# Key norms by one transpose and a row through DRAM, and low rotary keys on 128 partitions, in a diffusion backbone's attention

## Chip, cores and metric

One core of a Trainium2 chip runs the whole program. The metric is device time in microseconds (us) of one execution, as the median of several. Five engines work side by side, each through its own instructions in order: TensorE (PE, with its weight loads shown as PEld), VectorE (DVE), ScalarE (ACT), GpSimd (POOL) and SyncE (SP), which here only issues transfers.

## The reference, cut to what matters

Two layers over 512 latent tokens of width 1024, with 256 context tokens as a prefix. Layer 0 mixes tokens by latent attention with 8 heads, layer 1 by a gated MLP; a squared-ReLU MLP follows each. The change lies in layer 0's attention:

```python
kv = (rmsnorm(ckv, kv_a_norm) @ wkv_b).reshape(B, S, MLA_HEADS, QK_NOPE + V_DIM)
k_nope, v = kv[..., :QK_NOPE], kv[..., QK_NOPE:]
k_pe = jnp.broadcast_to(k_pe[:, :, None, :], (B, S, MLA_HEADS, QK_ROPE))
k = rmsnorm(jnp.concatenate([k_nope, k_pe], axis=-1), k_norm)
...
k_lat = rope_part(k_lat, cos, sin)
...
s = jnp.einsum('bqhd,bkhd->bhqk', qi, k, preferred_element_type=jnp.float32) * scale
p = jax.nn.softmax(s, axis=-1)
return jnp.einsum('bhqk,bkhd->bqhd', p.astype(v.dtype), v)
```

A key has 128 plain dimensions and 64 rotary ones, which all heads share. Each head divides its keys by a norm of its own, one number for each of the 768 tokens (256 context, 512 latent).

## The kernel before, in words

Every product is made from split operands: a float32 value is cut into a high part that the engine's fast format holds and a low part, the rest. A product is three matmuls (high by high, high by low, low by high: `mm3`, lines 80 to 82), and `split` (lines 72 to 76) makes the parts, the high one on ACT and the low one on DVE.

Attention runs from about 107 to 350 us of the span, with three generators for each head or pair of heads. `kv_proj(h)` projects head h's keys and values, token tile by token tile (six tiles of 128), transposes the keys (`kt`, line 265) and splits them into `kh` and `kl`. `q_proj(p)` does the same for the queries of two heads. `scores(h, half)` makes, for a tile of 128 queries, the 128 x 768 scores in one PSUM tile `s`, which has a single buffer: five pairs of matmuls of 384 columns (line 633), of which the last two use the rotary keys, `rh` (high) and `rl` (low). `values(h, half)` transposes the probabilities (`pt`, line 655), splits them into `th` and `tl` and multiplies them with the values into `o`.

The keys are not divided by their norms. Instead the scores are multiplied by `rk`, the reciprocal norms of the 768 keys, which must stand in all 128 partitions since the keys lie along a row of scores. One DVE instruction (line 637) multiplies `s` by `rk` and by the query's factor `rq` and finds the row's maximum; the exponential (ACT, line 640) and the scaling (DVE, line 642) follow. The next block of scores needs the buffer that line 637 reads.

The norms come in columns: `st[:, 2, t]` holds those of token tile t, one for each partition, from a sum of squares (ACT, line 260), an addition (DVE, line 270) and a power (POOL, line 271). Lines 272 to 277 spread them: for each token tile a float32 matmul takes the column, repeated 128 times, as the stationary operand and the identity as the moving one, which writes the column as a row into every partition. Two PSUM tiles of three such matmuls (`rkb`) are copied to `rk` by ACT.

The rotary keys are set up once, before the heads (lines 528 to 537): `kpe` holds them twice side by side, so that the transposed tile `krt` has the 64 dimensions in its lower and again in its upper 64 partitions. `rh` takes all 128 partitions, because the queries' rotary part `sq` has its high half in the lower and its low half in the upper 64. `rl` takes the lower 64 alone and meets only `sq`'s lower half.

What sets the order: a scheduler of the framework puts the instructions of each engine in order by its own estimate of their times, within what the data and the buffers allow. Loads of weights go through SP's queue (line 96), four raw buffers deep, each load behind the split that frees its buffer. A background task (`ada_steps`, lines 154 to 188) loads modulation weights through POOL's queue and sums them on DVE.

Of the kernel before, what the change touches and what calls it, by code (L numbers as in the profile page):

```python
# [9 lines left out]
F32 = mybir.dt.float32  # L10
F32R = mybir.dt.float32r
BF16 = mybir.dt.bfloat16
AF = mybir.ActivationFunctionType
ALU = mybir.AluOpType
AX = mybir.AxisListType

P = 128
# [4 lines left out]
TOK = CTX + SEQ  # L22
NT = TOK // P
NL = SEQ // P
HEADS = 8
NOPE = 128
ROPE = 64
# [19 lines left out]
def hybrid_dit_kernel(  # L47
# [6 lines left out]
    nc = tc.nc  # L54
    PE, ACT, DVE, POOL = nc.tensor, nc.scalar, nc.vector, nc.gpsimd
    SBUF, PSUM = bass.MemoryType.SB, bass.MemoryType.PSUM

    def pool(stack, name, bufs=1, space=SBUF, side="left"):
        return stack.enter_context(tc.tile_pool(name=name, bufs=bufs, space=space, side=side, reuse_waits="tile"))
# [19 lines left out]
    def mm3(o, wh, wl, mh, ml, start, stop):  # L79
        PE.matmul(o, lhsT=wh, rhs=mh, start=start, stop=False)  # L80
        PE.matmul(o, lhsT=wh, rhs=ml, start=False, stop=False)  # L81
        return PE.matmul(o, lhsT=wl, rhs=mh, start=False, stop=stop)  # L82
# [34 lines left out]
    ident = per.tile([P, P], F32, name="ident")  # L117
# [92 lines left out]
    ap_ = pool(att, "att")  # L210
# [2 lines left out]
    cq_h = ap_.tile([P, 3, SEQ], F32R, name="cq_h")  # L213
    cq_l = ap_.tile([P, 3, SEQ], F32R, name="cq_l")
    rh = ap_.tile([P, TOK], F32R, name="rh")
    rl = ap_.tile([ROPE, TOK], F32R, name="rl")
    epk = ap_.tile([P, NT], F32, name="epk")
    cosT = ap_.tile([P, NT, ROPE], F32, name="cosT")
    sinT = ap_.tile([P, NT, ROPE], F32, name="sinT")
# [15 lines left out]
    at = SimpleNamespace()  # L235
    Ks, Vs, Qs, Os = {}, {}, {}, {}
    HALF_T = SEQ // 2

    def kv_proj(h):
        wh, wl = at.W(wkv_b, 0, 2, h * 256, 256, f"wkb{h}")  # L240
        vh = at.hp.tile([P, NT, P], F32R, tag="vh", bufs=3, name=f"vh{h}")
        vl = at.hp.tile([P, NT, P], F32R, tag="vl", bufs=3, name=f"vl{h}")
        kh = at.hp.tile([P, TOK], F32R, tag="kh", bufs=2, name=f"kh{h}")
        kl = at.hp.tile([P, TOK], F32R, tag="kl", bufs=2, name=f"kl{h}")
        rk = at.hp.tile([P, TOK], F32, tag="rk", bufs=2, name=f"rk{h}")
        Ks[h], Vs[h] = (kh, kl, rk), (vh, vl)
        st = at.hp.tile([P, 3, NT], F32, tag="st", bufs=2, name=f"st{h}")
        T = None
        for u in range(3):
            t0 = 2 * u  # L250
            o = at.pm(f"kv{h}{u}").rearrange("p (t n) -> p t n", t=2)
            for j in range(2):
                s = slice((t0 + j) * P, (t0 + j + 1) * P)
                for k in range(2):
                    mm3(o[:, j, :], ckv_h[:, k, s], ckv_l[:, k, s], wh[:, k, :], wl[:, k, :], k == 0, k == 1)
            kn = at.hp.tile([P, 2, NOPE], F32, tag="kn", bufs=2, name=f"kn{h}{u}")
            ACT.copy(out=kn, in_=o[:, :, :NOPE])
            split(o[:, :, NOPE:], vh[:, t0:t0 + 2, :], vl[:, t0:t0 + 2, :])
            for j in range(2):
                ACT.activation(out=junk[:, :NOPE], in_=kn[:, j, :], func=AF.Square, accum_out=st[:, 0, t0 + j:t0 + j + 1])  # L260
            if u != 1:
                T = at.pt(f"kt{h}{u}")
            for j in range(2):
                i = j + 2 * (u == 1)
                PE.transpose(T[:, i * P:(i + 1) * P], kn[:, j, :], ident)
            if u:
                s = slice(0, 512) if u == 1 else slice(512, TOK)
                split(T[:, :s.stop - s.start], kh[:, s], kl[:, s], gqk)
            yield
        DVE.scalar_tensor_tensor(out=st[:, 1, :], in0=st[:, 0, :], scalar=1.0 / QK, in1=epk, op0=ALU.mult, op1=ALU.add)  # L270
        POOL.tensor_tensor(out=st[:, 2, :], in0=st[:, 1, :], in1=mhalf[:, :NT], op=ALU.pow)
        for u in range(2):
            o = at.pt(f"rkb{h}{u}")
            for j in range(3):
                t = 3 * u + j
                PE.matmul(o[:, j * P:(j + 1) * P], lhsT=st[:, 2, t:t + 1].to_broadcast([P, P]), rhs=ident, start=True, stop=True)
            ACT.copy(out=rk[:, u * 384:(u + 1) * 384], in_=o[:, :384])
        yield

    def q_proj(p):  # L280
# [6 lines left out]
        for u in range(2):  # L287
# [4 lines left out]
            for j in range(2):  # L292
# [13 lines left out]
                for h in range(2):  # L306
                    PE.transpose(T[:, h, j * P:(j + 1) * P], qn[:, h, :], ident)
            s = slice(u * HALF_T, (u + 1) * HALF_T)
            split(T, qh[:, :, s], ql[:, :, s])
# [8 lines left out]
            for h in range(2):  # L318
                ACT.copy(out=sq[h][:, s], in_=T[:, h * HALF_T:(h + 1) * HALF_T])
            us = slice(2 * u, 2 * u + 2)  # L320
# [11 lines left out]
    with ExitStack() as ini_stack:  # L332
# [7 lines left out]
        def pt(name):  # L340
            return ps.tile([P, 512], F32, tag="t", bufs=2, name=name)

        def pa(name):
            return ps.tile([P, 512], F32, tag="a", bufs=6, name=name)
# [60 lines left out]
        with ExitStack() as xstack:  # L405
# [12 lines left out]
            for k in range(0, KT, 2):  # L418
                o = pa(f"xct{k}")
# [4 lines left out]
            for k in range(KT):  # L424
                o = pa(f"xt{k}")
# [7 lines left out]
        for t in range(NT):  # L433
            o = rp[0][:, t * P:(t + 1) * P] if t < 2 else rp[1][:, (t - 2) * P:(t - 1) * P]
# [18 lines left out]
        for k in range(KT):  # L453
# [6 lines left out]
            for t in range(NT):  # L460
                a_h, a_l = (ch, cl) if t < 2 else (hh[k], hl[k])
                s = bass.ts(t if t < 2 else t - 2, P)
# [23 lines left out]
        for t in range(NT):  # L486
            st = ini.tile([P, 4], F32, name="kst", bufs=4)
# [7 lines left out]
            o = pt(f"ckt{t}")  # L495
            for j in range(2):
                PE.transpose(o[:, j * P:(j + 1) * P], ck[:, j * P:(j + 1) * P], ident)
            for j in range(2):
                s = slice(t * P, (t + 1) * P)
# [12 lines left out]
        for t in range(NL):  # L512
            o = pa(f"qa{t}")
            for k in range(KT):
                s = bass.ts(t, P)
# [3 lines left out]
            st = ini.tile([P, 4], F32, name="qst", bufs=4)  # L519
# [11 lines left out]
        for u in range(2):  # L531
            o = pt(f"krt{u}")
            for j in range(3):
                PE.transpose(o[:, j * P:(j + 1) * P], kpe[:, 3 * u + j, :, :].rearrange("p a r -> p (a r)"), ident)
            s = slice(u * 384, (u + 1) * 384)
            ACT.copy(out=rh[:, s], in_=o[:, :384])
            DVE.tensor_tensor(out=rl[:, s], in0=o[:ROPE, :384], in1=rh[:ROPE, s].bitcast(F32), op=ALU.subtract)

        drain(kv0)

# [2 lines left out]
    class Norm:  # L543
# [7 lines left out]
        def work(self, i, name):  # L551
            return per.tile([P, HALF_T], F32, tag=("nacc", "nsq")[i], bufs=NB[i], name=name)

        def add(self, k, half):
            name = self.name
            src = xT[:, k, half * HALF_T:(half + 1) * HALF_T]
            if self.acc[half] is None:
# [14 lines left out]
        def spread(self, half, pt):  # L572
            self.rb[half] = pt(f"{self.name}rb{half}")[:, :HALF_T]
            for t in range(2):
                PE.matmul(self.rb[half][:, t * P:(t + 1) * P], lhsT=self.st[half][:, 1, t:t + 1].to_broadcast([P, P]),
                          rhs=ident, start=True, stop=True)

        def apply(self, half, pt):
# [4 lines left out]
            if self.rb[half] is None:  # L583
                self.spread(half, pt)
            s = slice(half * HALF_T, (half + 1) * HALF_T)
            for k in range(KT):
# [17 lines left out]
    with hst as st_:  # L604
# [17 lines left out]
        def scores(h, half):  # L622
            kh, kl, rk = Ks[h]
            rk = rk.rearrange("p (a b) -> p a b", a=2)
            qh, ql, sq, rq_ = Qs[h // 2]
            i = h % 2
            for t in (2 * half, 2 * half + 1):
                s = slice(t * P, (t + 1) * P)
                S = ps.tile([P, 2, 512], F32, tag="s", bufs=PS, name=f"s{h}{t}")
                ops = [(qh[:, i, s], kh), (qh[:, i, s], kl), (ql[:, i, s], kh), (sq[i][:, s], rh), (sq[i][:ROPE, s], rl)]  # L630
                for m, (a, b) in enumerate(ops):
                    for n in range(2):
                        PE.matmul(S[:, n, :384], lhsT=a, rhs=b[:, n * 384:(n + 1) * 384], start=m == 0, stop=m == 4)  # L633
                sm = hq.tile([P, 4], F32, tag="sm", bufs=4, name=f"sm{h}{t}")
                rq = rq_[:, t, i, 2:3]
                e = hq.tile([P, 2, 384], F32, tag="p", bufs=5, name=f"p{h}{t}")
                DVE.tensor_tensor_reduce(out=e, in0=S[:, :, :384], in1=rk, op0=ALU.mult, op1=ALU.max, scale=rq,  # L637
                                         scalar=-3.0e38, accum_out=sm[:, 0:1])
                DVE.tensor_scalar(out=sm[:, 1:2], in0=sm[:, 0:1], scalar1=-1.0, scalar2=None, op0=ALU.mult)  # L639
                ACT.activation(out=e, in_=e, func=AF.Exp, bias=sm[:, 1:2], accum_out=sm[:, 2:3])  # L640
                DVE.reciprocal(out=sm[:, 3:4], in_=sm[:, 2:3])
                DVE.tensor_scalar(out=e, in0=e, scalar1=sm[:, 3:4], scalar2=None, op0=ALU.mult)  # L642
                Pr[h, t] = e.rearrange("p a b -> p (a b)")
# [185 lines left out]
    with ExitStack() as st_:  # L829
# [7 lines left out]
        for q in range(4):  # L837
            ws = [W(gm_w_in, 2 * k2, 2, HALF + q * 512, 512, f"gv{q}{k2}") for k2 in range(4)]
            for ts in ((0, 1), (2, 3)) if q == 0 else ((0, 1, 2, 3),):
                acc = {t: (pu if t < 2 else pd)(f"v{q}{t}") for t in ts}  # L840
                for k in range(KT):
                    wh, wl = ws[k // 2]
                    for t in ts:
                        s = slice(t * P, (t + 1) * P)
                        mm3(acc[t], hs[k][0][:, s], hs[k][1][:, s], wh[:, k % 2, :], wl[:, k % 2, :], k == 0, k == KT - 1)
                for t in ts:
# [8 lines left out]
                            in_=gm_bs.rearrange("g p -> (g p)").unsqueeze(0).to_broadcast([P, G * P]))  # L855
        for g4 in range(2):
            o = pt(f"wst{g4}")
# [6 lines left out]
            o = pt(f"rsw{g4}")  # L864
# [121 lines left out]
```

## Time and profile before

| | us |
|---|---|
| median of 3 runs | 1401.54 (1399.29 to 1401.88) |
| the profiled execution | 1399.21 |
| its span | 1397.4 |
| PE busy | 1355.4 |
| DVE busy | 856.0 |
| ACT busy | 545.6 |

The profiled execution is one run; durations and waits below are from it. A busy share tells which engine is full in a stretch; "idle before" and the releaser after an arrow tell what ended a wait. "issue" is time in which an engine waited for nothing that the profile shows. Matmuls are pipelined, so the step from one start to the next is what a matmul costs, not its record's length.

### The profile page before, as it was taken

Reading aid. Unit: us, or ns where it says so; the run is one execution under the profiler, and the core shown is the slowest. Engines: PE = TensorE matmul, PEld = TensorE weight load, DVE = VectorE, ACT = ScalarE, POOL = GpSimd, SP = SyncE. Lnnn points to the kernel's source line nnn. Section 1 sums busy time; section 2 is a strip of 40 time slices with the busy share of each in tenths; the row PEclk is TensorE's granted clock in tenths of the full one; section 3 lists DMA queues with packets and bytes.
Section 4 is the critical chain, followed back from the end, with each engine's and each line's share of the span. In section 5 each row is a group of like instructions: output and inputs, shape, how many; then the busy total and the mean of one; then the engine's idle time right before and its main releaser. Section 6 shows DMA issues by size and latency. Waiting matters only on the chain.

```text
span 1397.4 us, 18421 instructions
## 1 busy us (share of the span) xinstructions
PE 1355.4 (97%) x7159; PEld 1149.3 (82%) x7159; DVE 856.0 (61%) x1423; ACT 545.6 (39%) x1046; POOL 88.7 (6%) x140
## 2 busy tenths in 40 slices
PE   6989899999899999999999999999999999999998
PEld 4878889888898888888898888888888888888888
DVE  5876787887899888543457356555575344343442
ACT  6556556564652231322335233222254133231331
POOL 2031111100011111000000010000000000000000
PEclk9998999999999999999999999999999999999999
DMA  9551221311478878333323332222223222333311
GB/s 286 169 171 35 80 89 41 114 46 39 132 224 277 280 249 272 98 103 99 97 69 102 102 111 86 90 92 91 76 61 121 91 91 91 94 103 93 104 46 61
DMA packets 126823, 163.23 MB, mean 117 GB/s; under 512 B 7467, under 2 KB 111488, under 8 KB 126736
## 3 DMA queue, kind: packets, MB, share of 16 engines
q1 hardware_dynamic: 114784, 119.50, 27.0%
q0 software_dynamic: 11808, 42.03, 9.5%
q8 instruction: 56, 0.92, 0.3%
q10 hardware_dynamic: 144, 0.52, 0.1%
q14 instruction: 31, 0.25, 0.1%
HBM read 159.94 MB, written 2.10 MB: 116 GB/s over the span
## 4 chain that ended last, share of the span: by engine, by line
PE 85%; issue 7%; DVE 3%; DMA 2%; ACT 1%; POOL 1%; SPq 0%; POOLq 0%; DVEq 0%; ACTq 0%
PE s L633 3%; PE v L80 2%; PE v L82 2%; PE v L81 2%; DMA adr<-in_ada_w_dram 2%; PE pt L655 1%; PE wo L80 1%; PE f1d2o L82 1%; PE f1d0o L80 1%; PE f1d0o L81 1%; PE f1d2o L81 1%; PE f1d2o L80 1%; PE f1d0o L82 1%; PE f0d1o L80 1%; PE f0d1o L81 1%
## 5 line engine op out<-in xcount | busy, mean ns | idle before, releaser
L165 DVE SCALAR_TENSOR_TENSOR acc<-adr,sil,acc 128x1024 f32<-128x1024 f32 x70 | 89.7, 1281 | 20.7 <-DMA adr<-in_ada_w_dram 20.0
L161 POOL DMA_DIRECT2D adr<-in_ada_w_dram x80 | 43.4, 542 | 220.9 <-DVE acc L165 122.6
L782 DVE TENSOR_TENSOR f1a<-f1a 128x512 f32<-128x512 f32 (+1 forms) x36 | 22.5, 629 | 39.8 <-ACT f1a L781 39.8
L637 DVE CUSTOM_DVE_ANT_0 p<-s,rk,rq 128x768 f32<-128x768 f32 x32 | 32.5, 1015 | 14.1 <-PE s L633 11.9
L73 DVE TENSOR_TENSOR tl<-pt,th 128x512 fp32r<-128x512 f32 x48 | 32.7, 687 | 11.6 <-ACT th L72 11.2
L72 ACT CAST f0uh<-f0a 128x512 fp32r<-128x512 f32 (+1 forms) x36 | 20.4, 572 | 48.5 <-DVE f0a L782 48.5
L72 ACT CAST th<-pt 128x512 fp32r<-128x512 f32 x48 | 27.9, 589 | 23.6 <-PE o L82 13.6
L640 ACT ACTIVATE p<-p,sm 128x768 f32<-128x768 f32 x32 | 30.1, 940 | 15.1 <-DVE sm L639 15.1
L126 POOL TENSOR_TENSOR nst<-nst,mhalf 128x2 f32<-128x2 f32 x6 | 5.1, 854 | 457.5 <-DVE nst L125 457.5
L73 DVE TENSOR_TENSOR f1ul<-f1a,f1uh 128x512 fp32r<-128x512 f32 (+1 forms) x36 | 22.6, 632 | 18.8 <-ACT f1uh L72 18.6
L782 DVE TENSOR_TENSOR f0a<-f0a 128x512 f32<-128x512 f32 (+1 forms) x36 | 22.5, 627 | 18.4 <-ACT f0a L781 18.4
L72 ACT CAST f1uh<-f1a 128x512 fp32r<-128x512 f32 (+1 forms) x36 | 20.4, 572 | 32.0 <-DVE f1a L782 32.0
L73 DVE TENSOR_TENSOR f0ul<-f0a,f0uh 128x512 fp32r<-128x512 f32 (+1 forms) x36 | 22.4, 627 | 11.7 <-ACT f0uh L72 11.7
L81 PE MATMUL o<-tl,vh 128*128 128x256 f32 x96 | 28.1, 292 | 1.0 <-DVE tl L73 0.9
L80 PE MATMUL o<-th,vh 128*128 128x256 f32 x96 | 28.6, 298 | 0.0
L600 DVE SCALAR_TENSOR_TENSOR xT<-wo,mod,xT 128x512 f32<-128x512 f32 (+1 forms) x40 | 25.1, 638 | 5.2 <-PE wo L82 4.9
L655 PE MATMUL pt<-ident,p 128*128 128x128 f32 x192 | 27.7, 274 | 0.0
L82 PE MATMUL o<-th,vl 128*128 128x256 f32 x96 | 27.1, 282 | 0.0
L655 PEld LDWEIGHTS pt<-ident,p 128*128 128x128 f32 x192 | 22.2, 141 | 1.8 <-issue 1.0
L892 DVE TENSOR_TENSOR gm<-gm,u 128x512 f32<-128x512 f32 x16 | 11.0, 689 | 20.6 <-ACT u L873 20.5
L81 PEld LDWEIGHTS o<-tl,vh 128*128 128x128 f32 x96 | 18.2, 190 | 2.4 <-DVE tl L73 1.7
L642 DVE TENSOR_SCALAR p<-p,sm 128x768 f32<-128x768 f32 x32 | 19.8, 618 | 0.6
(2637 smaller groups left out, 4651.6 us busy)
## 6 DMA issues: line engine op xcount, KB each, us to landing
adr<-in_ada_w_dram POOLq DMA_DIRECT2D x80, 512.0 KB, 4.8
xn<-in_x_dram SPq DMA_DIRECT2D x4, 512.0 KB, 7.2
out_dram<-of SPq DMA_DIRECT2D x8, 256.0 KB, 2.2
xn<-in_ctx_dram SPq DMA_DIRECT2D x2, 512.0 KB, 4.1
ada000r<-in_ada_w_dram SPq DMA_DIRECT2D x1, 512.0 KB
ada001r<-in_ada_w_dram SPq DMA_DIRECT2D x1, 512.0 KB
ada100r<-in_ada_w_dram SPq DMA_DIRECT2D x1, 512.0 KB, 11.3
ada101r<-in_ada_w_dram SPq DMA_DIRECT2D x1, 512.0 KB, 10.2
```

The costliest lines, as they stand in the source:

```text
L72: ACT.copy(out=hi, in_=src)
L73: eng.tensor_tensor(out=lo, in0=src, in1=hi.bitcast(F32), op=ALU.subtract)
L80: PE.matmul(o, lhsT=wh, rhs=mh, start=start, stop=False)
L81: PE.matmul(o, lhsT=wh, rhs=ml, start=False, stop=False)
L82: return PE.matmul(o, lhsT=wl, rhs=mh, start=False, stop=stop)
L161: nc.gpsimd.dma_start(out=r, in_=ada_w[l][k * P:(k + 1) * P, ch * D:(ch + 1) * D])
L165: DVE.scalar_tensor_tensor(out=acc, in0=r, scalar=sil[:, k, 0:1], in1=acc, op0=ALU.mult, op1=ALU.add)
L633: PE.matmul(S[:, n, :384], lhsT=a, rhs=b[:, n * 384:(n + 1) * 384], start=m == 0, stop=m == 4)
L637: DVE.tensor_tensor_reduce(out=e, in0=S[:, :, :384], in1=rk, op0=ALU.mult, op1=ALU.max, scale=rq, scalar=-3.0e38, accum_out=sm[:, 0:1])
L640: ACT.activation(out=e, in_=e, func=AF.Exp, bias=sm[:, 1:2], accum_out=sm[:, 2:3])
L655: PE.transpose(T[:, j, q * P:(q + 1) * P], Pr[h, 2 * half + q][:, (2 * jp + j) * P:(2 * jp + j + 1) * P], ident)
L782: DVE.tensor_tensor(out=f, in0=f, in1=f, op=ALU.mult)
```

## The change

Line 274 now transposes the six columns of norms in one go: 128 x 6 becomes 6 x 128, in float32, by the identity. ACT copies this small tile to SBUF (`rr`), SP writes it to a DRAM tile `rkd` as one row of 768 numbers, and a second transfer reads that row into all 128 partitions of `rk`. The two transfers stand in SP's queue among the weight loads. The low rotary keys `rl` take all 128 partitions, and their matmuls use all 128 rows of `sq`, so the queries' low half now meets the low keys as well.

```diff
-    rl = ap_.tile([ROPE, TOK], F32R, name="rl")
+    rl = ap_.tile([P, TOK], F32R, name="rl")
...
+    rkd = pool(ctx, "rkd", space=bass.MemoryType.DRAM).tile([HEADS, TOK], F32, name="rkd")
...
         POOL.tensor_tensor(out=st[:, 2, :], in0=st[:, 1, :], in1=mhalf[:, :NT], op=ALU.pow)
-        for u in range(2):
-            o = at.pt(f"rkb{h}{u}")
-            for j in range(3):
-                t = 3 * u + j
-                PE.matmul(o[:, j * P:(j + 1) * P], lhsT=st[:, 2, t:t + 1].to_broadcast([P, P]), rhs=ident, start=True, stop=True)
-            ACT.copy(out=rk[:, u * 384:(u + 1) * 384], in_=o[:, :384])
+        o = at.pt(f"rkt{h}")
+        PE.transpose(o[:NT, :P], st[:, 2, :], ident)
+        row = at.hp.tile([NT, P], F32, tag="rr", bufs=2, name=f"rr{h}")
+        ACT.copy(out=row, in_=o[:NT, :P])
+        nc.sync.dma_start(out=rkd[h].rearrange("(t p) -> t p", p=P), in_=row)
+        nc.sync.dma_start(out=rk, in_=rkd[h].unsqueeze(0).to_broadcast([P, TOK]))
...
-            DVE.tensor_tensor(out=rl[:, s], in0=o[:ROPE, :384], in1=rh[:ROPE, s].bitcast(F32), op=ALU.subtract)
+            DVE.tensor_tensor(out=rl[:, s], in0=o[:, :384], in1=rh[:, s].bitcast(F32), op=ALU.subtract)
...
-                ops = [(qh[:, i, s], kh), (qh[:, i, s], kl), (ql[:, i, s], kh), (sq[i][:, s], rh), (sq[i][:ROPE, s], rl)]
+                ops = [(qh[:, i, s], kh), (qh[:, i, s], kl), (ql[:, i, s], kh), (sq[i][:, s], rh), (sq[i][:, s], rl)]
```

The scheduler makes a new order for the whole attention stage. Three places show it. Names carry buffer numbers here, and behind the diff's added lines the code stands one line lower.

PE at head 1, from the norms' spreading to the head's first block of scores, before (`rkb`: spread norms; `pt`: transposed probabilities of head 0; `s`: scores):

```order
L276 MATMUL rkb_1496<-ident,st_1424 128x128 x3
L276 MATMUL rkb_1501<-ident,st_1424 128x128 x3
L655 MATMUL pt_1545<-ident,p_1389 128x128
...
L655 MATMUL pt_1545<-ident,p_1407 128x128
L633 MATMUL s_1592<-kh_1421,qh_1231 128x384 x2
```

and of the change:

```order
L274 MATMUL rkt_1495<-ident,st_1423 6x128
L656 MATMUL pt_1540<-ident,p_1388 128x128
...
L656 MATMUL pt_1540<-ident,p_1406 128x128
L656 MATMUL pt_1555<-ident,p_1388 128x128
...
L656 MATMUL pt_1555<-ident,p_1406 128x128
L634 MATMUL s_1587<-kh_1420,qh_1230 128x384 x2
```

Six matmuls became one transpose, and a second tile of four transposed probabilities moved ahead of the scores.

DVE at head 3, from the split of a weight to the first multiply with the head's norms (L637 before, now L638; printed as ISA), before:

```order
L600 SCALAR_TENSOR_TENSOR xT<-wo_2300,mod,xT 128x512
L73 TENSOR_TENSOR wo02l<-wo02r,wo02h 128x512
L637 ISA p_2320,sm_2319<-s_2308,rk_2111,rq_1894 128x768
L637 ISA sm_2319 128x1
L73 TENSOR_TENSOR tl_2239<-pt_2233,th_2238 128x512
```

and of the change:

```order
L73 TENSOR_TENSOR tl_2226<-pt_2220,th_2225 128x512
L73 TENSOR_TENSOR tl_2241<-pt_2235,th_2240 128x512
L601 SCALAR_TENSOR_TENSOR xT<-wo_2391,mod,xT 128x512
L601 SCALAR_TENSOR_TENSOR xT<-wo_2399,mod,xT 128x512
L73 TENSOR_TENSOR wqb20l<-wqb20r,wqb20h 128x384
L638 ISA p_2307,sm_2306<-s_2295,rk_2102,rq_1885 128x768
L638 ISA sm_2306 128x1
L73 TENSOR_TENSOR tl_2256<-pt_2250,th_2255 128x512
```

Two splits of probabilities, two residual additions and a weight's split now stand ahead of the multiply.

SP's queue at heads 1 to 3 (a piece of the difference):

```order
 L96 DMA wkb4r<-in_mla_wkv_b_dram 128x2x256
+L277 DMA rkd<-rr_1497 6x128
+L278 DMA rk_1422<-rkd 128x768
+L277 DMA rkd<-rr_1766 6x128
+L278 DMA rk_1691<-rkd 128x768
 L96 DMA wo02r<-in_mla_wo_dram 128x2x256
 L96 DMA wqb20r<-in_mla_wq_b_dram 128x384
 L96 DMA wqb21r<-in_mla_wq_b_dram 128x384
 L96 DMA wqb22r<-in_mla_wq_b_dram 128x384
+L277 DMA rkd<-rr_2177 6x128
 L96 DMA wo03r<-in_mla_wo_dram 128x2x256
+L278 DMA rk_2102<-rkd 128x768
```

Each head's write and read stand in line with the weight loads; head 3's read is behind the load wo03r.

## Rows read from the trace of the kernel before

**Rows 1.** The page, part 1: busy us (share of the span) xinstructions

```profile
PE 1355.4 (97%) x7159; PEld 1149.3 (82%) x7159; DVE 856.0 (61%) x1423; ACT 545.6 (39%) x1046; POOL 88.7 (6%) x140
```

**Rows 2.** Stretches: us, busy (xinstructions) PE, PEld, DVE, ACT, POOL; clock, DMA, GB/s

```profile
100.00:125.00 25.00, 21.66 (x116) 20.09 (x116) 15.67 (x49) 13.61 (x50) 3.64 (x3) 0.73 0.20 58
150.00:175.00 25.00, 21.04 (x147) 19.21 (x146) 21.15 (x49) 14.58 (x45) 5.51 (x7) 1.00 0.36 104
...
sum 175.00, PE 174.81 PEld 155.70 DVE 138.70 ACT 98.71 POOL 18.00; mean PE 24.97 PEld 22.24 DVE 19.81 ACT 14.10 POOL 2.57
```

**Rows 3.** Line 633: ns min/median/max, starts; then idle before it (us, times)

```profile
L633 PEld LDWEIGHTS s<-rh,sq x64: 187/188/192, 124.3 to 347.4; 128*128 128x128 f32 x64
L633 PEld LDWEIGHTS s<-rl,sq x64: 182/184/187, 124.9 to 347.9; 64*128 64x128 f32 x64
...
  issue: 7.8, 32
```

**Rows 4.** Order of time on PE, one block: start us, us, instruction [idle before <-releaser]

```profile
252.87 0.51 PE L633 MATMUL s<-kh,ql 128*128 128x384 f32 x2
253.22 0.51 PE L633 MATMUL s<-rh,sq 128*128 128x384 f32 x2
253.66 0.61 PE L633 MATMUL s<-rl,sq 64*128 64x384 f32 x2
254.20 0.38 PE L80 MATMUL o<-th,vh 128*128 128x256 f32 x1
254.42 0.28 PE L81 MATMUL o<-tl,vh 128*128 128x256 f32 x1
254.54 0.28 PE L82 MATMUL o<-th,vl 128*128 128x256 f32 x1
```

**Rows 5.** The same block's weight loads (PEld)

```profile
253.66 0.29 PEld L633 LDWEIGHTS s<-rl,sq 64*128 64x128 f32 x2 [0.25 <-issue]
```

**Rows 6.** Order of time on PE at head 0's and head 3's spread norms

```profile
108.78 2.93 PE L276 MATMUL rkb<-ident,st 128*128 128x128 f32 x12 [0.89 <-POOL st L271]
...
197.37 1.50 PE L276 MATMUL rkb<-ident,st 128*128 128x128 f32 x12
198.70 0.60 PE L655 MATMUL pt<-ident,p 128*128 128x128 f32 x4
199.06 0.48 PE L80 MATMUL wo<-oh,wo01h 128*128 128x512 f32 x1
199.37 0.39 PE L81 MATMUL wo<-ol,wo01h 128*128 128x512 f32 x1
199.60 0.39 PE L82 MATMUL wo<-oh,wo01l 128*128 128x512 f32 x1
```

**Rows 7.** Order of time on PE at head 2: rows after a wait

```profile
163.08 1.60 PE L276 MATMUL rkb<-ident,st 128*128 128x128 f32 x12 [1.91 <-POOL st L271]
...
171.77 0.62 PE L633 MATMUL s<-kh,qh 128*128 128x384 f32 x2 [1.35 <-ACT qh L72]
...
173.43 0.39 PE L81 MATMUL o<-tl,vh 128*128 128x256 f32 x1 [0.69 <-DVE tl L73]
```

**Rows 8.** Transfers: issuer, count, KB each, us to landing; last, the output's writes

```profile
wqa4r<-in_mla_wq_a_dram SPq DMA_DIRECT2D x1, 384.0 KB, 3.2
...
cosT<-in_rope_cos_dram SPq DMA_DIRECT2D x1, 192.0 KB, 9.1
...
bsb<-in_gm_bs_dram ACTq DMA_DIRECT2D x1, 512.0 KB, 5.0
...
DMA to landing us min/median/max: 2.1/2.2/2.9
```

**Rows 9.** Order of time at head 1: SP's load, ACT's copy, DVE's multiply

```profile
140.01 0.37 SPq L96 DMA_DIRECT2D wkb4r<-in_mla_wkv_b_dram  x1
...
140.60 0.48 ACT L277 COPY rk<-rkb 128x384 f32<-128x384 f32 x1 [0.27 <-PE rkb L276]
...
143.66 1.02 DVE L637 CUSTOM_DVE_ANT_0 p<-s,rk,rq 128x768 f32<-128x768 f32 x1 [0.65 <-PE s L633]
```

## The prediction

> **What bounds the kernel now.** I read the page's busy shares first: TensorE (PE) is busy 97% of the span [rows 1]. A share over the whole span says nothing about one stage, so I then read the busy times by stretch. The attention stage, about 107 to 350 us, is where every changed line runs. From 175 to 350 us PE is busy 174.8 of 175 us, while VectorE (DVE) has 138.7 and ScalarE (ACT) 98.7 [rows 2]. So in seven tenths of the stage a microsecond taken off PE is a microsecond off the end, unless something else becomes late. Two stretches are different. From 100 to 125 us PE runs at a granted clock of 0.73, and from 150 to 175 us it has about 4 us of idle time [rows 2]. Next come the rows of the two touched operations, and last the landing times of transfers like the two that are added.
>
> **Low rotary keys on 128 partitions.** This edit looks like nothing: the two matmuls of each block still stream 384 columns. The trace shows that they cost more than their neighbours. In the line's own view the weight loads of the 64-row form sit behind 7.8 us of "issue" time, in 32 of 32 blocks [rows 3]. One block in order of time shows the size. The 128-row pairs of 384 columns start 0.35 us apart (252.87 to 253.22). The next pair, the 64-row one, starts 0.44 us later, at 253.66, and the 256-column matmul behind it another 0.54 us later, at 254.20 [rows 4]. That one itself takes 0.22 us to its follower, where its kin take 0.12 [rows 4]. So the block is late by 0.09 + 0.19 + 0.10 = 0.38 us. Before the 64-row load PE's weight path stood idle for 0.25 us [rows 5]: the loads that normally run under the matmul ahead don't, at the change from 128 rows to 64 and again on the way back. With 128 rows there is no change of form, so I take 32 x 0.38 = **12.2 us** off PE. The bounds are 7.8 us (the booked idle time alone) and twice that.
>
> The Trainium skill, TensorEngine Tiling, Key Properties, says that a change of tiling mode drains the TensorE; the 0.25 us row is what such a drain would look like.
>
> DVE's subtraction into the low keys is twice as many partitions and the same 384 columns. It runs twice in all, so I price it at nothing.
>
> **The norms' broadcast.** Before, each head runs six f32 matmuls, recorded as twelve, in 1.33 us at the full clock (197.37 to the next start at 198.70) [rows 6]. Eight heads are 10.6 us. Head 0's take 2.93 us at the slow clock [rows 6]. I still count 1.33 for it: the matmuls behind it move up into the slow stretch and pay there. The new transpose is one pass over 128 columns. Four such transposes and a 512-column matmul take 0.67 us (198.70 to 199.37), and the 512-column matmul is 0.23, so one transpose is 0.11 us [rows 6], and eight are 0.9 us. That leaves 9.7 us. But its stationary operand has 6 columns, a form that this stage has nowhere else. Its change of form could cost nothing, or as much as the 64-row one. The trace has no clean row for it, and I take the nearest, the 0.38 us of rows 4, for each of eight heads: **3.0 us** back (0 to 3.0). In head 2 the gain is lost. PE waits 1.91 us for GpSimd's power before its matmuls there, and then idles 1.35 and 0.69 us for ACT and DVE within the next 11 us [rows 7]. Finishing earlier only lengthens those waits: **1.2 us** (1.33 - 0.11) back. ACT loses sixteen copies of 0.48 us [rows 9] and gets eight of 6 rows; it is not the bound, and I count nothing.
>
> **The new wait.** In place of two copies from PSUM the row now goes out to DRAM and comes back to all partitions, both on SyncE's queue, the second issued when the first has landed. Who waits is DVE, whose multiply of the scores with the norms (L637) stands in a strict order, and behind it PE, because the scores have a single buffer: the next block of scores starts only when that multiply is done. From the transpose I count 0.3 us for it, 0.4 for ACT's small copy, 2.2 for the write (the output's writes: 2.1 to 2.9), 3.2 for the read (a 384 KB load; a 512 KB broadcast from DRAM took 5.0) [rows 8], and 1.0 for the multiply [rows 9]: 7.1 us, with 2.9 and 5.0 instead 9.6 us. What hides it is PE's own work between the transpose and the second block of scores of that head. The changed order has, for head 1, 20 transposes, 13 matmuls of 384 columns and 13 of 256: 20 x 0.11 + 13 x 0.175 + 13 x 0.118 = 6.0 us. Counted so, heads 3, 5 and 7 have 8.8, 9.1 and 9.1 us; the old order had 4.7, 4.3, 6.6 and 4.3 us. The even heads are projected a whole head ahead of their use (head 2's matmuls run at 163 us [rows 7], its first scores' start at 171.77), and have 10 us or more. So only head 1 stalls, by 7.1 - 6.0 = **1.1 us**; at 9.6 the four odd heads stall by 3.6 + 0.8 + 0.5 + 0.5 = 5.4 us, at less than 6.0 none.
>
> SyncE's queue is passed sixteen times. Ahead of head 1's write stands the load wkb4r, which waited for its buffer until 140.01 us, when head 1's copies were just starting (140.60) [rows 9]: no delay. Behind the new entries stand weight loads; the next one after head 1's and 2's, wo02r, went out only at 170 us before, because its buffer was taken. A few microseconds of blocked queue there are hidden.
>
> **The new order.** Hundreds of PE rows change places in this stage, and a little outside it. DVE has 138.7 us of work in 175 [rows 2]; with some 12 us fewer it is at 85%, and waits like those in rows 7 become more likely. I charge one more such pair, 1.35 + 0.69 = **2.0 us** (0 to 8.0, two more stretches with 4 us idle like 150 to 175).
>
> **Sum.** 12.2 + 9.7 - 3.0 - 1.2 - 1.1 - 2.0 = 14.6 us. The profiled execution took 1399.2 us, 1.8 more than its span, so 1384.6; the median of the three runs lies 2.3 us above that execution, which makes 1386.9. I put the forecast at **1386**.
>
> **Rivals.**
> First, nothing is given back: the six-column form drains nothing, no wait and no reordering costs. Then 12.2 + 9.7 = 21.9 us go, 1377. For it: PE is full, and three of four odd heads have cover. Against it: head 2's idle time is in the trace.
>
> Second, the widened keys bring nothing, because the 0.38 us has another cause than the row count (the last matmul of a block, the bank it closes). Then 14.6 - 12.2 = 2.4 us go: 1396.8, with the median's offset 1399, no change that can be measured. For it: those matmuls are also the last of each block, so position and row count can't be told apart in this trace. Against it: the idle time lies on the load before them as well as behind.
> The Trainium skill, TensorE: Matmul & The Clock Gate, Part 2, has a rule on this side: a weight load's time follows its columns, not its rows. By that rule alone a 64-row matmul costs what a 128-row one does and this is the result; the loads' own lengths agree with it (184 and 188 ns [rows 3]), the idle time ahead of them does not.
>
> Third, slower: the round trip through DRAM outlasts the cover. The deciding point: the gain before stalls is 15.7 us, the four odd heads' cover 33.0 us, so the chain must be (33.0 + 15.7) / 4 = 12.2 us, its two landings 10.5 us instead of 5.4. One load of the start (cosT, 192 KB) did take 9.1 us [rows 8]. With 2.9 and 9.1 the chain is 13.7 us, the stalls 7.7 + 4.9 + 4.6 + 4.6 = 21.8 us, and the time 1399.2 + 6.1 = 1405. Against it: of the transfers in rows 8 only that one, at the start with the queues full, took over 5.0 us.
>
> **How the numbers follow.** Forecast 0.65, first rival 0.14, second 0.10, third 0.11. About 0.2% (2.8 us) is what a measurement of this kernel can tell from no change. Forecast and first rival are faster; the second falls within 0.2%; with a little of the forecast's weak edge moved there, that is 0.79, 0.10, 0.11. The worst of the bounds together, 12.2 + 6.7 - 1.2 - 5.4 - 8.0 = 4.3 us, gives 1395, with the median's offset 1397; the best is 1377. The range 1377 to 1398 leaves out the third rival and the edges.
>
> **What would show it.** In the changed profile: no "issue" time before the low-key matmuls, and 0.35 us from their start to the next (12.2); eight short transposes with or without idle time ahead and behind (3.0); DVE's wait at L637 (now one line lower) for a transfer, long in head 1 and short or none in 3, 5 and 7; PE still full from 175 us on. It is wrong if PE's idle time in 107 to 350 us grows by more than 10 us, or if the low-key matmuls keep their gap.

## The result, and the profile after

The changed kernel takes 1386.37 us (median of 4 runs, 1386.17 to 1387.54), beside 1401.71 us (4 runs) before: a ratio of 0.9897, with a 95% interval of 0.9885 to 0.9910. That is 15.3 us by the medians, 14.4 by the ratio (12.6 to 16.1). The forecast was 1386 in a range of 1377 to 1398. The profiled execution took 1386.22 us, its span 1384.4, 13.0 less than before.

The page's first part, against [rows 1]: busy us (share of the span) xinstructions.

```profile
PE 1335.3 (96%) x7071; PEld 1140.3 (82%) x7071; DVE 852.6 (62%) x1423; ACT 538.7 (39%) x1038; POOL 89.0 (6%) x140
```

PE lost 20.1 us of busy time, but the span only 13.0 us: some of what was freed turned into waiting. The busy times by stretch show where, against [rows 2] (columns as there):

```profile
100.00:125.00 25.00, 17.93 (x101) 16.68 (x101) 17.37 (x55) 14.98 (x59) 4.83 (x6) 0.86 0.29 93
125.00:150.00 25.00, 23.56 (x167) 22.94 (x166) 16.41 (x43) 16.93 (x50) 1.33 (x2) 1.00 0.15 48
150.00:175.00 25.00, 21.62 (x148) 19.72 (x147) 21.50 (x53) 16.09 (x50) 5.72 (x8) 1.00 0.39 118
175.00:350.00 175.00, 171.62 (x1159) 161.37 (x1158) 146.44 (x338) 100.94 (x286) 17.98 (x19) 1.00 0.25 79
```

From 175 to 350 us PE was busy 174.8 of 175 us before and is 171.6 now. (The last 15 us of it are already other work, since the stage ends earlier.) One block of scores on PE, against [rows 4] (start, us, instruction):

```profile
128.40 0.51 PE L634 MATMUL s<-kh,ql 128*128 128x384 f32 x2
128.75 0.51 PE L634 MATMUL s<-rh,sq 128*128 128x384 f32 x2
129.10 0.51 PE L634 MATMUL s<-rl,sq 128*128 128x384 f32 x2
129.45 0.60 PE L317 MATMUL qrt<-ident,qs 128*128 128x128 f32 x4
```

Every pair takes 0.35 us from its start to the next, the low keys' too. That holds beyond this block: before, the step into the low keys' pair has a median of 0.44 us and the step out of it 0.54 over all 32 blocks; both are 0.35 now. Line 634's list of what ended the idle time before it, against [rows 3], has no issue time left, and a wait for DVE's multiply in its place:

```profile
  DVE sm L638: 10.1, 10
  ACT qh L72: 0.3, 1
```

That multiply, line 638, waits for the transfer four times (us, times):

```profile
  DMA rk<-rkd: 9.2, 4
```

Below I compare kernels by stage, since the parts ahead of attention and behind it differ by 1 to 4 us from profile to profile. The marks are starts of instructions in order of time: the first and the last of DVE's 32 multiplies of the scores, and PE's first matmul of the MLP that follows. PE idle is the sum of the gaps on PE between the first and the last multiply. Us, worked out from the traces; the kernels of the lower rows are those of the experiments.

| kernel | start to first multiply | first to last | last to the MLP | MLP to the end | PE idle, first to last |
|---|---|---|---|---|---|
| before | 125.7 | 222.8 | 27.1 | 1021.9 | 4.1 |
| changed | 126.5 | 208.3 | 26.6 | 1023.0 | 8.0 |
| changed, again | 126.4 | 209.1 | 26.6 | 1022.8 | 7.8 |
| wide keys alone | 126.2 | 211.1 | 26.9 | 1021.0 | 3.3 |
| row norms alone | 127.3 | 216.6 | 26.8 | 1028.3 | 6.1 |
| no round trip | 124.7 | 204.4 | 26.9 | 1023.5 | 5.2 |
| transpose on DVE | 122.7 | 206.8 | 24.9 | 1022.1 | 5.7 |

The gain of the change lies in the third column: 14.5 us.

### The profile page after: what moved, and what is told of

Read it like the earlier page. It is cut to its first block, busy times and chain, and to the rows that moved or that the text cites. A ratio compares the mean times of both kernels' runs of the same rounds, so it can differ in the third digit from the quotient of the medians.

```text
span 1384.4 us, 18271 instructions
## 1 busy us (share of the span) xinstructions
PE 1335.3 (96%) x7071; PEld 1140.3 (82%) x7071; DVE 852.6 (62%) x1423; ACT 538.7 (39%) x1038; POOL 89.0 (6%) x140
## 4 chain that ended last, share of the span: by engine, by line
PE 78%; DVE 6%; DMA 5%; issue 5%; ACT 2%; POOL 1%; DVEq 0%; POOLq 0%; ACTq 0%
DMA adr<-in_ada_w_dram 5%; PE s L634 3%; PE v L80 2%; PE v L82 2%; PE v L81 2%; DVE acc L165 2%; PE f1d2o L80 1%; PE f1d0o L81 1%; PE f1d0o L82 1%; PE f1d0o L80 1%; PE f1d2o L81 1%; PE f1d2o L82 1%; PE f1d1o L80 1%; PE f0d2o L80 1%; PE f0d2o L81 1%
## 5 line engine op out<-in xcount | busy, mean ns | idle before, releaser
L638 DVE CUSTOM_DVE_ANT_0 p<-s,rk,rq 128x768 f32<-128x768 f32 x32 | 32.5, 1014 | 13.5 <-DMA rk<-rkd 9.2
L72 ACT CAST th<-pt 128x512 fp32r<-128x512 f32 x48 | 27.1, 587 | 18.8 <-PE o L82 12.6
L82 PE MATMUL o<-th,vl 128*128 128x256 f32 x96 | 27.1, 282 | 0.0
L656 PE MATMUL pt<-ident,p 128*128 128x128 f32 x192 | 26.8, 273 | 0.0
L634 PE MATMUL s<-kh,qh 128*128 128x384 f32 x64 | 17.6, 357 | 4.3 <-DVE sm L638 4.2
```

What stands on the lines that cost most here:

```text
L72: ACT.copy(out=hi, in_=src)
L656: PE.transpose(T[:, j, q * P:(q + 1) * P], Pr[h, 2 * half + q][:, (2 * jp + j) * P:(2 * jp + j + 1) * P], ident)
```

## Experiments

### Each edit alone

The scheduler's order does not depend on the low keys' rows: with wide keys alone the order of PE, DVE, ACT and SP's transfers is that of before, row for row, and with the row norms alone that of the changed kernel. So these two kernels part the edits cleanly.

```diff
-    rl = ap_.tile([ROPE, TOK], F32R, name="rl")
+    rl = ap_.tile([P, TOK], F32R, name="rl")
...
-(sq[i][:ROPE, s], rl)]
+(sq[i][:, s], rl)]
```

> The kernel before with the low rotary keys on 128 partitions and nothing else; the order of TensorE is that of before, row for row. Theory: the change of form between 128 and 64 rows costs 0.38 us in each of 32 blocks, so 12.2 us go, 1401.7 to 1389.5, and the step from the low keys' start to the next matmul is 0.35 us. Rival (the last pair of a block is late whatever its rows): 1401.7, and the steps of 0.44 and 0.54 us stay. A second rival: the saved time turns into waits for VectorE, PE's busy time falls by some 12 us but the end by much less, 1395 or later.

Measured: 1388.19 us, ratio 0.9923 (0.9903 to 0.9944), so 10.8 us (7.8 to 13.6) less than before; 11.8 in the stage. The steps are 0.35 us (one block of this kernel on PE):

```profile
125.17 0.51 PE L633 MATMUL s<-rh,sq 128*128 128x384 f32 x2
125.53 0.52 PE L633 MATMUL s<-rl,sq 128*128 128x384 f32 x2
125.88 0.28 PE L80 MATMUL kv<-wkb1h,ckv_h 128*128 128x256 f32 x1
```

PE's idle time in the stage did not grow (4.1 to 3.3 us). The wide keys bring what the theory says, and they bring it to the end.

The other half, the changed kernel with the low keys back on 64 rows:

```diff
-    rl = ap_.tile([P, TOK], F32R, name="rl")
+    rl = ap_.tile([ROPE, TOK], F32R, name="rl")
...
-(sq[i][:, s], rl)]
+(sq[i][:ROPE, s], rl)]
```

> The changed kernel with the low rotary keys back on 64 partitions; the order of TensorE is that of the changed kernel. Theory: the norms' edit gives what the whole change gave less 12.2 us, that is 15.3 - 12.2 = 3.1 us, 1398.6. By the terms on record without the six-column form's 3.0 us it would be 5.4 us, 1396.3; with them 2.4 us, 1399.3. Rival (the norms' edit is the whole gain): 1386.4. Rival (VectorE's waits for the row become longer or shorter when PE is slower): the waits of heads 1, 3, 5 and 7 at the multiply, 4.0, 0.2, 2.8 and 2.1 us in the changed kernel, shrink where PE runs later.

Measured: 1394.37 us, ratio 0.9959 (0.9945 to 0.9973), 5.7 us (3.8 to 7.7) less than before; 6.2 in the stage. (Its profiled execution took 1400.76, 6.4 over its median, and the excess is behind the stage: 1028.3 us where the other kernels have 1021.0 to 1023.5.) It came out near the 5.4 us of the terms without the six-column form's charge. The two edits alone give 11.8 + 6.2 = 18.0 us in the stage, together 14.5 (13.7 in the repeat): 3.5 us are lost when both stand. Of these, 2.7 us are idle time of PE: against before it falls by 0.8 with the wide keys alone and grows by 1.9 with the row norms alone, but by 3.8 with both. Half of that goes with the round trip: PE's gaps behind the late multiplies of heads 1 and 5 are 1.8 us here and 3.2 in the changed kernel, whose PE is earlier and meets the same round trip, while DVE's four waits for the transfer are 7.8 us in sum here and 9.2 there. The rest of the 3.5 I can't place.

### Row count or position

The kernel before, with the 64-row pair third of five:

```diff
-(qh[:, i, s], kl), (ql[:, i, s], kh), (sq[i][:, s], rh), (sq[i][:ROPE, s], rl)]
+(qh[:, i, s], kl), (sq[i][:ROPE, s], rl), (ql[:, i, s], kh), (sq[i][:, s], rh)]
```

> The kernel before, with the pair of the low rotary keys (64 rows) as third of the five pairs of a block instead of last. The result is the same sum in another order. Theory (row count): the steps of 0.44 us ahead of the 64-row pair and 0.54 behind its start go with it to the middle, the last pair (now the high rotary keys, 128 rows) has 0.35 us to its follower, and the time stays at 1401.7, within 0.2%. Rival (position): the 64-row pair takes 0.35 us in the middle, and the delay stays with the last pair of the block.

One block of it on PE, and the same block's weight loads (in brackets: idle before):

```profile
257.33 0.51 PE L633 MATMUL s<-kl,qh 128*128 128x384 f32 x2
257.77 0.61 PE L633 MATMUL s<-rl,sq 64*128 64x384 f32 x2
258.32 0.61 PE L633 MATMUL s<-kh,ql 128*128 128x384 f32 x2
258.77 0.51 PE L633 MATMUL s<-rh,sq 128*128 128x384 f32 x2
259.12 0.28 PE L80 MATMUL o<-th,vh 128*128 128x256 f32 x1
```

```profile
257.77 0.29 PEld L633 LDWEIGHTS s<-rl,sq 64*128 64x128 f32 x2 [0.25 <-issue]
258.31 0.30 PEld L633 LDWEIGHTS s<-kh,ql 128*128 128x128 f32 x2 [0.25 <-issue]
258.60 0.36 PEld L633 LDWEIGHTS s<-rh,sq 128*128 128x128 f32 x2
```

The delay went with the 64-row pair: 0.44 us ahead of it, 0.55 from its start, 0.45 for the pair behind, in place of 0.35 each, so 0.39 us in all; and 0.25 us without a weight load on the way into the form and again on the way out. The last pair, now of 128 rows, has 0.35 us to its follower. The delay does not stay with the last position. The time was not what I expected: 1404.63 us, ratio 1.0034 (1.0017 to 1.0050), 4.8 us slower than before where I wrote within 0.2%; 2.3 us of it are in the stage. The scheduler made a new order for this kernel, which moved DVE's and ACT's rows too, and I can't say which of them costs it.

How many rows make another form? The changed kernel with the low keys on 96 partitions:

```diff
-    rl = ap_.tile([P, TOK], F32R, name="rl")
+    rl = ap_.tile([96, TOK], F32R, name="rl")
...
-(sq[i][:, s], rl)]
+(sq[i][:96, s], rl)]
```

> The changed kernel with the low rotary keys on 96 partitions. Same order. Theory A (any matmul with fewer rows than its neighbours changes form): 0.38 us in 32 blocks come back, 1386.4 + 12.2 = 1398.6. Theory B (only a tile of 64 rows or fewer is another form; 96 rows still take the whole array): 1386.4, and 0.35 us from the low keys' start to the next matmul.

Measured: 1385.54 us, ratio 0.9896 (0.9879 to 0.9913), that of the changed kernel. Here are the line's two rows of 96 (its idle list has no issue time):

```profile
L634 PEld LDWEIGHTS s<-rl,sq x64: 187/189/193, 125.6 to 334.0; 96*128 96x128 f32 x64
L634 PE MATMUL s<-rl,sq x64: 334/338/344, 125.8 to 334.1; 96*128 96x384 f32 x64
```

96 rows go like 128. Not fewer rows as such cost the 0.39 us, but the form of 64. (Other row counts were not run.)

### What the round trip costs

The changed kernel, with a second transfer that waits for nothing (it reads other numbers, so the result leaves the norms out):

```diff
-        nc.sync.dma_start(out=rk, in_=rkd[h].unsqueeze(0).to_broadcast([P, TOK]))
+        nc.sync.dma_start(out=rk, in_=rope_cos.rearrange("a b -> (a b)")[:TOK].unsqueeze(0).to_broadcast([P, TOK]))
```

> The changed kernel, but the second transfer reads 768 numbers of an input in place of the row just written, so that the multiply has no round trip to wait for; the keys' norms are left out of the result. The transpose, the small copy, the write and a read of the same size remain. Theory: of the round trip only head 1's 1.45 us of idle TensorE and small waits beside it reach the end, so 1386.4 falls by 1.5 to 2.5 us, to about 1384.5, and VectorE's 9.2 us of waits for the transfer go. Rival (all of the 3.8 us by which TensorE's idle time in the stage grew come from the round trip): 1382.6 or less. Rival (nothing of it reaches the end): 1386.4.

Measured: 1382.05 us, ratio 0.9870 (0.9855 to 0.9886), so about 3 to 4 us less than the changed kernel (0.9897, and 0.9891 in its repeat). The stage is 4.0 us shorter (4.7 than the repeat's), PE's idle time in it 2.7, and DVE's waits for the transfer are gone; all that its multiply still waits for is PE (us, times):

```profile
  PE s L634: 5.0, 10
```

By the time, the rival was right and my theory (1.5 to 2.5 us) too low. But the scheduler made a new order for this kernel too, so the 3 to 4 us are the wait and the order made around it together; 2.7 of the 3.8 us by which PE's idle time grew go with them. The changed kernel's own trace gives 3.2 us: the sum of PE's four gaps that a late multiply ended at heads 1 and 5. I had counted only the wait that PE meets first, at head 1. A later one is at head 5, one block behind the multiply that waited:

```profile
264.12 1.02 DVE L638 CUSTOM_DVE_ANT_0 p<-s,rk,rq 128x768 f32<-128x768 f32 x1 [2.83 <-DMA rk<-rkd]
...
271.51 0.61 PE L634 MATMUL s<-kh,qh 128*128 128x384 f32 x2 [1.00 <-DVE sm L638]
```

PE waited only 0.28 us behind the multiply of 264 us, but DVE, 2.83 us behind by then, worked without a gap up to its next multiply (270.43 us) and was late for PE's block at 271. The kernel without the round trip has neither gap.

A longer chain: the row goes once more from DRAM to DRAM.

```diff
-        nc.sync.dma_start(out=rk, in_=rkd[h].unsqueeze(0).to_broadcast([P, TOK]))
+        nc.sync.dma_start(out=rke[h].rearrange("(t p) -> t p", p=P), in_=rkd[h].rearrange("(t p) -> t p", p=P))
+        nc.sync.dma_start(out=rk, in_=rke[h].unsqueeze(0).to_broadcast([P, TOK]))
```

> The changed kernel with one more transfer in the chain: the row is copied from DRAM to DRAM before it is read to all partitions. The chain of 7.7 us at head 1 grows by some 2.2 us or more. Theory (the cover counts: 6.3 us at head 1, near 9 at the other odd heads): TensorE's stall at head 1 grows from 1.45 by the whole added time, the other odd heads stall by 1 to 2 us each, so some 3 to 8 us in all, 1389 to 1394. Rival (VectorE and the new order hide it): 1386 to 1388. Rival (transfers queue up behind one another on SyncE and weights come late): idle time of TensorE before matmuls of weights, over 1395.

Measured: 1387.88 us, ratio 0.9914 (0.9895 to 0.9933), 1.5 us over the changed kernel by the medians and 2.4 by the ratio, with intervals that overlap; 211.4 us in the stage, 3.0 more. My theory (1389 to 1394) was wrong, and the time is the first rival's. The added transfer took 1.9 to 4.0 us from its issue to the read's. DVE's four waits for the read did not grow (8.7 us, after 9.2): the scheduler, which counts the added transfer, made a new order with other work ahead of the multiplies. PE's idle time grew to 8.8, its stall at head 1 from 1.4 to 2.1. So the cover is not a fixed number of matmuls, as my working had it: it is what the scheduler puts there.

### Too long, and shorter

Columns straight to DRAM, in pieces of 4 bytes:

```diff
-        PE.transpose(o[:NT, :P], st[:, 2, :], ident)
...
-        nc.sync.dma_start(out=rkd[h].rearrange("(t p) -> t p", p=P), in_=row)
+            nc.sync.dma_start(out=rkd[h].rearrange("(t p) -> p t", p=P), in_=st[:, 2, :])
```

> The changed kernel without transpose and small copy: the norms go from their columns straight to the DRAM row, 768 pieces of 4 bytes, and from there to all partitions as before. TensorE loses eight transposes (0.9 us) and its waits for GpSimd's power at heads 0 and 2 (1.15 and 1.90 us), and the chain starts 1 to 3 us earlier. Theory (the write of small pieces takes no more than 2 us longer than the row's 2.1 to 3.4): 3 to 5 us less than the changed kernel, 1382. Rival (small pieces are slow, the write takes 6 us or more): the stall at head 1 grows to 4 us or more, 1387 to 1395.

Measured: 1418.26 us, ratio 1.0110 (1.0073 to 1.0147): slower than before by far more than the 0.3% of the kernel with the pair in the middle, and 23 us over the rival's upper end. The page's count of packets, first of the changed kernel, then of this one:

```profile
DMA packets 128070, 166.38 MB, mean 120 GB/s; under 512 B 7643, under 2 KB 111712, under 8 KB 127984
```

```profile
DMA packets 134246, 166.38 MB, mean 117 GB/s; under 512 B 13867, under 2 KB 117888, under 8 KB 134160
```

Some 6200 small packets more, which is about eight times 768. SP's queue at head 1, first of the changed kernel, then of this one; the read is issued when the write has landed:

```profile
140.51 0.30 SPq L277 DMA_DIRECT2D rkd<-rr  x1
142.64 0.35 SPq L278 DMA_DIRECT2D rk<-rkd  x1
```

```profile
134.80 0.37 SPq L274 DMA_DIRECT2D rkd<-st  x1
144.66 0.34 SPq L275 DMA_DIRECT2D rk<-rkd  x1
145.09 0.39 SPq L96 DMA_DIRECT2D wkb4r<-in_mla_wkv_b_dram  x1
```

The same 3 KB take 2.1 us as six rows and 9.9 us as 768 pieces (8.4 to 14.8 over the heads), and the weight load wkb4r stands behind it. DVE then waits, and PE behind DVE:

```profile
148.88 1.02 DVE L635 CUSTOM_DVE_ANT_0 p<-s,rk,rq 128x768 f32<-128x768 f32 x1 [8.17 <-DMA rk<-rkd]
149.96 1.00 PE L631 MATMUL s<-kh,qh 128*128 128x384 f32 x2 [5.54 <-DVE sm L635]
```

This is the prediction's third rival as a kernel: the two landings of head 1 take 9.9 + 4.2 = 14.1 us, over its deciding point of 10.5, and the kernel is slower than before. But the round trip is not all of it. At head 2 PE waits for DVE, and DVE for another transfer, a load of the background task (`adr`):

```profile
171.49 1.28 DVE L165 SCALAR_TENSOR_TENSOR acc<-adr,sil,acc 128x1024 f32<-128x1024 f32 x1 [5.83 <-DMA adr<-in_ada_w_dram]
```

```profile
173.48 0.58 PE L81 MATMUL o<-tl,vh 128*128 128x256 f32 x1 [5.06 <-DVE tl L73]
```

The loads of this task that were under way beside the writes of heads 2 and 5 took 6.4 to 13.4 us to land, all but one of them over 8; in the changed kernel's stage they take 3.9 to 6.0. DVE's waits for them sum to 18.7 us here and to 3.1 there, those for the read to 26.3 and 9.2. In or right behind PE's five gaps of 2.9 us and more the granted clock falls from 2.4 to 1.2 GHz, for 37.6 us of the stage in all, where the changed kernel stays at 2.4 from 115 to 361 us. So the small pieces also made other transfers late, and the gaps cost clock.

The Trainium skill, DMA: Bandwidth & Descriptors, Specifications, gives 512 B as the least size of a piece for the full rate. The 4-byte pieces agree; the 128-byte ones of the next kernel, in a transfer this small, land as the 512-byte rows do. Whether the size of the pieces or their number costs the time, no run separates.

A shorter chain: DVE transposes the norms in squares of 32 x 32, so that neither PE nor ACT is in it, and the write moves 128 pieces of 128 bytes.

```diff
+    rkd = pool(ctx, "rkd", space=bass.MemoryType.DRAM).tile([HEADS, 32, 4, 32], F32, name="rkd")
+    stp = ap_.tile([P, 32], F32, name="stp")
+    POOL.memset(stp, 0.0)
...
-        POOL.tensor_tensor(out=st[:, 2, :], in0=st[:, 1, :], in1=mhalf[:, :NT], op=ALU.pow)
-        o = at.pt(f"rkt{h}")
-        PE.transpose(o[:NT, :P], st[:, 2, :], ident)
-        row = at.hp.tile([NT, P], F32, tag="rr", bufs=2, name=f"rr{h}")
-        ACT.copy(out=row, in_=o[:NT, :P])
-        nc.sync.dma_start(out=rkd[h].rearrange("(t p) -> t p", p=P), in_=row)
-        nc.sync.dma_start(out=rk, in_=rkd[h].unsqueeze(0).to_broadcast([P, TOK]))
+        POOL.tensor_tensor(out=stp[:, :NT], in0=st[:, 1, :], in1=mhalf[:, :NT], op=ALU.pow)
+        row = at.hp.tile([P, 32], F32, tag="rr", bufs=2, name=f"rr{h}")
+        DVE.transpose(out=row, in_=stp)
+        nc.sync.dma_start(out=rkd[h].rearrange("t b i -> b t i"), in_=row)
+        nc.sync.dma_start(out=rk, in_=rkd[h].rearrange("t b i -> (t b i)")[:TOK].unsqueeze(0).to_broadcast([P, TOK]))
```

> The changed kernel, with VectorE's transpose of 32 x 32 squares in place of TensorE's transpose and ACT's copy; the write puts 128 pieces of 128 bytes to DRAM, the read is the same row of 768 numbers. TensorE neither waits for GpSimd's power (1.15 us at head 0, 1.90 at head 2) nor spends 0.1 us eight times, and at head 1 the chain starts at the power's end, some 2.6 us earlier. Theory (the waits of the round trip reach the end with about 4 us, by the run without it): about half of these and the 0.9 us go, 1386.4 to 1382 or 1383. Rival (what is saved at head 2 is waited for behind it, as before the change, and VectorE's own queue delays the transpose): within 1 us of the changed kernel. Rival (128 small pieces land late, as the 768 of 4 bytes did): the write takes over 5 us, 1390 or later.

> The changed kernel itself once more, beside the runs of this call, to see how far its time and its stages differ from one profile to the next: 1386.4, a ratio of 0.990 to the kernel before, 208.3 us from the first to the last multiply of the scores within 1 us, and VectorE's four waits for the transfer at heads 1, 3, 5 and 7 within 0.5 us each.

Measured side by side: 1378.37 us, ratio 0.9844 (0.9830 to 0.9857), beside 1385.34 us, ratio 0.9891 (0.9876 to 0.9906), for the changed kernel again. This version beats both, by about 21 and 7 us. Its chain at head 1, on DVE and SP:

```profile
133.96 0.20 DVE L276 STREAM_TRANSPOSE rr<-stp 128x32 f32<-128x32 f32 x1
...
139.94 1.02 DVE L638 CUSTOM_DVE_ANT_0 p<-s,rk,rq 128x768 f32<-128x768 f32 x1 [0.64 <-PE s L634]
```

```profile
134.19 0.54 SPq L277 DMA_DIRECT2D rkd<-rr  x1
136.22 0.34 SPq L278 DMA_DIRECT2D rk<-rkd  x1
```

GpSimd's power starts at 132.09 us and takes 1.32; the transpose stands 0.55 us behind its end, where TensorE's stood 2.6 us behind. The multiply waits for PE, not for the transfer. Over all heads it waits for the transfer twice, 3.9 us, nearly all of it at head 5. The gain of 7 us is more than the 3 to 4 expected, and the scheduler made a new order here as well. Between this profile and the repeat of the changed kernel the span differs by 8.2 us: 3.7 ahead of the first multiply, 2.3 in the stage, 2.3 behind it. The part in the stage is what the theory speaks of; 2.1 of it are idle time of PE. Of the part ahead, 1.15 us is PE's wait for the power of head 0; the rest of it and the part behind belong to the new order of the program, and no run separates them. The repeat itself came out as the first time: 209.1 us in the stage, DVE's four waits 10.6 us in sum after 9.2 (the two at heads 5 and 7 each 0.7 longer, a little over the 0.5 I had allowed).

## Why the prediction was right, and where only its sum was

The total, 14.6 us, fell within the measured 12.6 to 16.1. Term by term:

**12.2 for the wide keys** held: alone they gave 10.8 us (7.8 to 13.6), 11.8 in the stage, and the delay read from one block, 0.38 us, is 0.39 where the form stands in the middle. The second rival (position), to which I gave 0.10, fell. The loads' lengths (188 and 184 ns [rows 3]) agree with the Trainium skill, TensorE: Matmul & The Clock Gate, Part 2, by which a load's time follows its columns; the matmuls' steps do not follow from it (0.44 and 0.54 us against 0.35). What the Trainium skill, TensorEngine Tiling (Array Packing), Key Properties, says on draining at a change of mode agrees with the gap of 0.25 us; that it is such a drain, no run shows.

**9.7 for the norms' matmuls** held as busy time: with the row norms alone PE's time in the stage fell by 6.2 us while its idle time grew by 1.9, so 8.1 of work went, where seven heads at 1.22 are 8.5. (Head 0's lies ahead of the first multiply, where the differences from profile to profile hide it.)

**3.0 back for the six-column form** was wrong; it is nothing. Head 3's transpose on PE, then on the weight path:

```profile
195.98 0.40 PE L82 MATMUL wo<-oh,wo00l 128*128 128x512 f32 x1
196.22 0.28 PE L274 MATMUL rkt<-ident,st 128*6 128x128 f32 x1
196.33 1.03 PE L656 MATMUL pt<-ident,p 128*128 128x128 f32 x8
```

```profile
195.99 0.08 PEld L274 LDWEIGHTS rkt<-ident,st 128*6 128x6 f32 x1
196.22 0.91 PEld L656 LDWEIGHTS pt<-ident,p 128*128 128x128 f32 x8
```

0.24 us from the 512-column matmul to it and 0.11 us from it to the next: no form change is paid, and the loads run under the matmul ahead. I had taken the nearest row, that of fewer rows, for a case of fewer columns. For a form of few columns the rule of the Trainium skill, TensorEngine Tiling (Array Packing), Key Properties, is not borne out, if that form counts as a mode of its own.

**1.2 back at head 2** is open. The wait for GpSimd's power is still there:

```profile
163.00 0.27 PE L274 MATMUL rkt<-ident,st 128*6 128x128 f32 x1 [1.91 <-POOL st L272]
```

The gaps from there to 184 us sum to 4.4 us (1.9, 0.7, 0.3, 1.0, 0.5). That is 1.2 more than with the wide keys alone (3.2), as charged, but only 0.4 more than in [rows 7] (4.0); and the row norms alone have 4.0 too, where 1.2 more was to be seen.

**1.1 back for the round trip** was the step that failed: it is 3 to 4 (3.2 in PE's gaps, 3 to 4 by the ratios; 4.0 to 4.7 in the stage, with the other order). The place was right, and the first stall nearly so:

```profile
146.40 1.02 DVE L638 CUSTOM_DVE_ANT_0 p<-s,rk,rq 128x768 f32<-128x768 f32 x1 [4.00 <-DMA rk<-rkd]
147.48 0.62 PE L634 MATMUL s<-kh,qh 128*128 128x384 f32 x2 [1.44 <-DVE sm L638]
```

From the transpose at 139.75 to the multiply's end the chain is 7.7 us (7.1 predicted), and PE had 6.3 us of other work (6.0 predicted); it stalls 1.44 us. What the step left out is that DVE stands in order behind its own wait. It waited 4.0, 0.2, 2.8 and 2.1 us at heads 1, 3, 5 and 7, where I had said short or none for the last three. PE's cover held at the first block there (a stall of 0.28 us at head 5, none at 3 and 7). The reads took 4.3 us as a median (3.2 to 5.2), not 3.2, and at head 5 the chain was 9.6 us, the length of my upper bound. DVE's work behind a wait is then late for PE in a later block, as the 1.00 us at 271 us shows.

**2.0 back for the new order** can't be told apart from head 2's: the last three of the gaps above stand where the kernel before has none, and in the kernel without the round trip too. Of the 8.0 us of PE's idle time in the stage 4.4 are these gaps and 3.2 the four that go with the round trip (1.44, 0.45, 0.27, 1.00); 0.4 are left, after 0.2 before. So head 2 and the new order, charged 3.2 together, come to some 0.7 us of idle time.

So some 5.5 us that I charged were not paid (3.0 and 2.5), and 2 to 3 of the round trip were not charged. PE's work in the stage fell by 18.3 us, where the first two terms come to 20.3 there (31 of the 32 blocks, seven of the eight heads); these 2 us I can't place. The errors nearly cancel, and that is luck: the forecast was better than its parts. Two bounds on record also do not follow from their terms. The worst sum has 12.2 for the wide keys, where their own lower bound of 7.8 would leave nothing of the 4.3 us; and the first rival's 1377 leaves out the median's offset of 2.3 us that the forecast has.

Of what was to show it: the issue time went, the steps are 0.35 us, and the short transposes have no idle time but for the power. PE is not full from 175 us on (171.6 of 175), as I had expected it to be; its idle time in the stage grew by 3.8 us, under the 10 that would have refuted the reading.

## What to carry to other kernels

Look at the form printed with each matmul: a pair of 64 rows between full ones cost 0.39 us more here than a full pair, and widening its operands is allowed if the added products belong to the sum or are zero. When a wait is put on an engine that works in order, charge not only who is waiting there first, but all that stands behind it on that engine: take the sum of its waits, not only the first stall of the full engine, as the bound. When a small tensor goes through DRAM, count the pieces of the write and the engines in the chain; the chain without PE and ACT made the faster kernel here, though its write carries 16 KB in place of 3.

## What was not expected of the hardware

A matmul of 96 rows runs in the same steps as one of 128 and without issue time; a pair of 64 rows between them costs 0.39 us more, on the way in and out. A transposing matmul with a stationary operand of six columns costs 0.11 us and nothing at its borders (read at head 3). A write of 3 KB took 1.2 to 3.4 us to the issue of the read behind it as six rows of 512 bytes (up to 4.0 in the repeat), 1.9 to 3.3 as 128 pieces of 128 bytes (which carry 16 KB), and 8.4 to 14.8 as 768 pieces of 4 bytes, beside which loads of the background task took up to 13.4 us instead of at most 6.0 in the changed kernel's stage.
